# An encoder block on one Trainium2 core: the sums that seven-product pairs share move from SBUF into PSUM banks, and the step lists are rewritten around them

## The chip, the core and the metric

The kernel runs on one core of a Trainium2 chip. Five engines with queues of their own take part: TensorE (PE in the profile; PEld are its weight loads) multiplies out of SBUF into the eight banks of PSUM, VectorE (DVE) and ScalarE (ACT) do the elementwise work, GpSimd (POOL) here only issues DMAs that add to what lies in SBUF, and SyncE (SP) issues all other DMAs. Each engine goes through its instructions strictly in the order in which the program lists them; an instruction that waits holds up all behind it. The metric is the device time in microseconds, median of several runs.

## What is computed

One layer of a transformer-like encoder, on 256 tokens of width 2048, all in float32:

```
h     = rms_norm(x);  q,k,v of three mixers and three gates = h @ w_in
a,b,c = dilated-window attention, grouped attention with rotary, cross-attention into 256 memory tokens
x     = x + (sum over i of sigmoid(gate_i) * (branch_i @ w_br_i)) @ w_o
x     = x + (silu(hf[:, :5632]) * hf[:, 5632:]) @ w_ffn_out,   hf = rms_norm(x) @ w_ffn_in
```

Nearly all of the work is products of a 256-row activation with weights that are read once from memory (295 MB in all). To keep float32's precision on TensorE, every operand is split into a high part (`whi`, `xh`) and the rest (`wlo`, `xl`), and every product of a 128x128 block of activations with a 128x512 block of weights is made of three matmuls: high by high, high by low, low by high.

## The kernel before

Weights arrive in blocks of two K-blocks by 512 columns (512 KB), over SP's queue, in eight places called `raw`. For each block ACT copies the high part (`whi`, line 397) and DVE subtracts it for the low part (`wlo`, line 407), 128x1024 elements each. `halves` takes the two from five buffers in turn, so the high part of a step cannot be made before TensorE has finished the step five before it.

The large products go two column blocks at a time, as a "pair" (`pair`, line 409): column blocks c=0 and c=1, two token blocks of 128, and eight or more pairs of K-blocks. Most pairs of K-blocks are done plainly, as "wholes": step `d` (for c=0) or `D` (for c=1) is one 512 KB block, 12 matmuls. The others are done as "sevens": a 2x2x2 block product by seven block multiplications in place of eight, with sums of activations (`forms`, made once for each activation and kept) and sums of weight blocks. Each pair has four result chains that grow in PSUM (mmY, mmV, mmZ, mmQ) and two shared chains: mmX, to which the products with three different sums are added one after the other, and mmW. After each of three phases mmX is copied by ACT into SBUF (tiles SA and SB, line 448); the shared sums are made there by DVE (lines 552, 555), and at the end of a pair DVE adds them to the four chains (`sums`, line 456), before the gate's sigmoid, the silu or the residual addition reads them. Sums of weights are made 512 wide by DVE (lines 506, 507, 513, 529) into tiles t2 and t3; the addition of the first two blocks is a DMA that POOL issues and that accumulates 256 KB into a loaded block (line 485).

The stages in order of time: memory keys and values (0 to 51 us), the projection to queries, keys and values with attention beside it (to 286), the first gate products (to 314), `merging` (to 580; pairs of gates, each followed by the branch products that they multiply), `projecting` (to 670; w_o in two pairs), `feeding` (to 1364; eleven pairs for the FFN's input in three groups of 4, 4 and 3, and after each group two pairs for its output). In a pair of `feeding`, `hidden` takes silu of one column block, multiplies it with the other, and transposes the product on TensorE (tiles `tp`) for the output pairs.

What sets the order: a list of steps for each kind of pair, such as `STEPS_FFN`, is a string of step names. `run` walks through it: it emits the high part's copy of a step four steps ahead of its products, the low part one step behind the high part, and after each step `tick` lets side jobs (evacuations, transposes, activation sums) emit a piece. `nc.follow` keeps ACT's and DVE's weight work in that order. PSUM's eight banks are two tags of four in one pool.

## Time and profile before

| | |
|---|---|
| runs (3) | 1368.52, 1368.80, 1369.07 us; median 1368.8 |
| the profiled execution's span | 1368.0 us |
| PE busy | 1358.7 us (99%), 6195 instructions |
| DVE busy | 1190.5 us (87%), 1652 instructions |
| ACT busy | 865.4 us (63%) |
| DMA | 298.86 MB, mean 218 GB/s |
| granted TensorE clock | full in each of 40 slices |

The profiled execution is as long as the runs within 0.1%. Matmuls are pipelined: a record lasts 0.39 us while the next begins 0.23 us later, so "busy" says only that TensorE never stood still for long; how fast it goes is read from the spacing of the starts.

### The profile page before, as it was taken

To read this page: it belongs to the slowest core of one execution; us is meant where nothing else is said; L and a number is where in the kernel's file an instruction comes from. 1 tells how busy PE (TensorE), PEld (TensorE's weight loads), DVE (VectorE), ACT (ScalarE), POOL (GpSimd) and SP (SyncE) were. 2 spreads that over 40 slices of the span, in tenths; PEclk is the share of its full clock that TensorE was granted. 3 is DMA by queue.
4 is the path that set the end of the run, shared out by engine and by line. 5 is a ranking of instruction groups with operands and counts; after the bars stand their busy time and mean duration, and the time that the engine had idled before them with its cause. 6 is when DMAs were issued, how large, how long until landed. Compare 5 with 4: busy or idle time off the path is not lost.

```text
span 1368.0 us, 17866 instructions
## 1 busy us (share of the span) xinstructions
PE 1358.7 (99%) x6195; PEld 1125.7 (82%) x6195; DVE 1190.5 (87%) x1652; ACT 865.4 (63%) x1152; POOL 85.1 (6%) x97
## 2 busy tenths in 40 slices
PE   9999999999999999999999999999999999999998
PEld 7888888888888888887878888888888888888887
DVE  6868877759889888878999998989999989899998
ACT  7777665646665565656776666655666765566754
POOL 0010000000000100000000010000001000011000
PEclk9999999999999999999999999999999999999999
DMA  9976445557776775954777777777787767787673
GB/s 366 343 234 203 151 156 168 171 166 225 239 237 201 225 242 180 308 181 146 242 223 220 233 211 221 220 246 212 222 247 218 230 187 243 217 247 225 204 224 108
DMA packets 91674, 298.86 MB, mean 218 GB/s; under 512 B 10368, under 2 KB 12928, under 8 KB 91328
## 3 DMA queue, kind: packets, MB, share of 16 engines
q1 hardware_dynamic: 79488, 275.94, 60.2%
q0 software_dynamic: 11952, 21.76, 9.7%
q8 instruction: 48, 0.79, 0.2%
q14 instruction: 42, 0.34, 0.1%
q10 hardware_dynamic: 144, 0.02, 0.0%
HBM read 294.81 MB, written 2.88 MB: 218 GB/s over the span
## 4 chain that ended last, share of the span: by engine, by line
PE 86%; DVE 8%; issue 2%; DMA 2%; ACT 1%; SPq 0%; DVEq 0%; ACTq 0%
PE mm L77 16%; PE mmZ L77 14%; PE mmV L77 14%; PE mmY L77 14%; PE mmQ L77 11%; PE mmX L77 10%; DVE wlo L407 4%; PE mmW L77 3%; DMA raw<-in_w_ffn 2%; PE tp L77 1%; ACT whi L397 1%; PE sc L77 1%; PE o L77 1%; DVE t L506 1%; PE pT L77 1%
## 5 line engine op out<-in xcount | busy, mean ns | idle before, releaser
L397 ACT ACTIVATE whi<-raw 128x1024 fp32r<-128x1024 f32 (+1 forms) x460 | 479.4, 1051 | 350.6 <-PE mmV L77 109.6
L407 DVE TENSOR_TENSOR wlo<-raw,whi 128x1024 fp32r<-128x1024 f32 (+1 forms) x460 | 546.8, 1210 | 80.7 <-ACT whi L397 77.5
L77 PE MATMUL mm<-whi,xT 128*128 128x512 f32 x640 | 202.5, 393 | 0.0
L131 DVE TENSOR_TENSOR wlo<-raw,whi 128x1024 fp32r<-128x1024 f32 x82 | 102.1, 1248 | 43.6 <-ACT whi L130 42.9
L77 PEld LDWEIGHTS mm<-whi,xT 128*128 128x128 f32 x640 | 119.3, 188 | 23.5 <-issue 0.4
L130 ACT ACTIVATE whi<-raw 128x1024 fp32r<-128x1024 f32 x82 | 86.7, 1061 | 62.3 <-PE mm L77 45.4
L77 PE MATMUL mm<-wlo,xT 128*128 128x512 f32 x320 | 125.7, 393 | 0.0
L407 DVE TENSOR_TENSOR wlo<-t,whi 128x1024 fp32r<-128x1024 f32 x90 | 102.2, 1138 | 13.4 <-ACT whi L397 12.9
L397 ACT ACTIVATE whi<-t 128x1024 fp32r<-128x1024 f32 x90 | 89.0, 990 | 25.5 <-PE mmQ L77 11.4
L77 PE MATMUL mmX<-whi,forms 128*128 128x512 f32 x312 | 104.9, 389 | 0.0
L77 PE MATMUL mmY<-whi,x1T 128*128 128x512 f32 x266 | 96.7, 394 | 0.8 <-DVE x1T L134 0.8
L77 PE MATMUL mmV<-whi,x1T 128*128 128x512 f32 x266 | 91.3, 390 | 0.0
L77 PEld LDWEIGHTS mm<-wlo,xT 128*128 128x128 f32 x320 | 60.2, 188 | 12.3 <-issue 0.7
L77 PEld LDWEIGHTS mmX<-whi,forms 128*128 128x128 f32 x312 | 58.6, 188 | 12.3 <-ACT SB L448 0.2
L485 POOL DMA_DIRECT2D raw<-in_w_ffn x43 | 37.2, 865 | 441.0 <-DMA raw<-in_w_ffn 143.3
L77 PE MATMUL mmZ<-whi,x1T 128*128 128x512 f32 x180 | 63.0, 391 | 0.0
L77 PE MATMUL mmQ<-whi,x1T 128*128 128x512 f32 x180 | 62.8, 390 | 0.0
L77 PE MATMUL mmW<-whi,forms 128*128 128x512 f32 x156 | 61.6, 395 | 0.0
L77 PE MATMUL mmZ<-whi,forms 128*128 128x512 f32 x156 | 60.9, 390 | 0.0
L77 PE MATMUL mmX<-wlo,forms 128*128 128x512 f32 x156 | 60.8, 389 | 0.0
L77 PEld LDWEIGHTS mmY<-whi,x1T 128*128 128x128 f32 x266 | 50.0, 188 | 11.3 <-DVE x1T L134 1.2
L507 DVE TENSOR_TENSOR t<-t,raw 128x512 f32<-128x512 f32 x83 | 57.1, 688 | 1.6
(285 smaller groups left out, 2837.9 us busy)
## 6 DMA issues: line engine op xcount, KB each, us to landing
raw<-in_w_ffn SPq DMA_DIRECT2D x176, 512.0 KB, 4.7
raw<-in_w_gate SPq DMA_DIRECT2D x96, 512.0 KB, 4.4
raw<-in_w_ffn_out SPq DMA_DIRECT2D x88, 512.0 KB, 4.6
raw<-in_w_qkv SPq DMA_DIRECT2D x64, 512.0 KB, 4.3
raw<-in_w_o SPq DMA_DIRECT2D x32, 512.0 KB, 4.8
raw<-in_w_br SPq DMA_DIRECT2D x24, 512.0 KB, 4.2
raw<-in_w_ffn POOLq DMA_DIRECT2D x43, 256.0 KB, 5.5
raw<-in_w_mem SPq DMA_DIRECT2D x15, 512.0 KB, 8.3
```

The source lines that it names most:

```text
L77: ins = op(*args, **kw)
L130: nc.scalar.activation(hi, src, AF.Copy)
L131: nc.vector.tensor_sub(lo, src, hi.bitcast(F32))
L397: nc.follow(nc.scalar.activation(hi[:, o], v, AF.Copy))
L407: nc.follow(nc.vector.tensor_sub(*due.pop(0)))
L485: nc.gpsimd.dma_start(out=b2[:, 0], in_=src(u, 0)[:, :NC], accum_op=ALU.add)
L506: nc.follow(nc.vector.tensor_add(s2, b2[:, 0], b2[:, 1]))
L507: nc.follow(nc.vector.tensor_sub(s3, s2, b1[:, 0]))
```

## The change

Seven-product pairs get a new plan. Sevens now come in doubles (four sevens to a pair, two in the w_o pairs), and every step of a double handles the same phase of two sevens: step kinds X, W, P, Y, Q, Z, H, each one 128x1024 block of weights or of their sums and 6 matmuls; `l` and `r` start loads. The shared sums stay in PSUM. When the last X step is through, ACT copies mmX into the bank that becomes mmY (line 514); when the last W step is through, ACT copies mmW to SBUF (`m5`, line 517); when the last P step is through, DVE writes m5 minus mmX back into mmW (line 519); when the last Q step is through, DVE writes m5 minus mmX into a new bank mmQ (line 523). The four banks mmY, mmX, mmW, mmQ are then the results, the chains go on on top, and readers (sigmoid, silu, residual) read PSUM directly. Tiles SA and SB and their additions are gone. The sums of weights are 128x1024 wide on DVE (lines 537, 539, 541), and the accumulating DMA is 512 KB (line 495): 46 issues for 83.

Each pair has three lists: front, back, end. The column block c=1 (mmW, mmQ) is finished within the pair; the end list holds wholes of c=0 (mmY, mmX) that fill the places marked "." in the next pair's front. The number of sevens is larger than before: the program has 27 matmuls of 128x512 fewer for products, and 2 more that only mark the two copied banks in the first such pair. A new PSUM pool over the same eight banks is opened before that pair: four banks for c=0, two for c=1, two for transposes. There are eleven `raw` places instead of eight. The activations' sums are made for four K-blocks at a time, and those of the first activation earlier, beside the second gate product.

```diff
-STEPS_GATE = "d4 d0 D0 f1 g1 d5 D5 f2 d6 g2 D4 f3 h1 g3 p0 p2 D6 q0 h3 q2 d7 D7".split()
-STEPS_FFN = "d0 D0 d1 D1 f2 f3 d5 g2 D5 g3 h2 f4 d6 g4 p0 p2 h4 D6 q0 q2 d7 D7".split()
...
+STEPS_GATE = ("l0 l1 X0 . X1 . . r0 W0 r1 W1 P0 P1 . Y0 Y1 . Q0 Q1 .", "Z0 Z1 D4 H0 D5 H1 d4 D6 d5 D7 d6 d7", "")
...
+STEPS_FFN = ("l0 l1 X0 X1 . r0 W0 r1 W1 P0 P1 . Y0 Y1 . Q0 Q1 .", "Z0 Z1 D4 H0 D5 H1 D6 D7", "d4 d5 d6 d7")
+STEPS_LAST = ("l0 l1 X0 X1 . r0 W0 . r1 W1 . P0 P1 . Y0 Y1 Q0 Q1", "Z0 Z1 H0 H1 D4 D5", "d4 d5")
...
     def bank(name, tag="at"):
-        return psum.tile([P, NC], F32, name=name, tag=tag)
+        return psum[0].tile([P, NC], F32, name=name, tag=tag, bufs=2 if tag in ("c1", "tp") else 4)
...
-        def copy(to, b):
-            with tc.high_priority():
-                nc.scalar.activation(tl[to[0]][:, to[1]], ps[b], AF.Copy)
-
-        def sums(c):
-
-            if not seven or parts:
-                return [ps[b] for b in ("YV", "ZQ")[c]]
-            to = tl["AB"[c]]
-            for t in range(T):
-                nc.vector.tensor_add(to[:, t], ps[("YV", "ZQ")[c][t]], to[:, t])
-            return to
+        def ending():
+            for c, (a, b) in enumerate(("YX", "WQ")):
+                if left[a] == left[b] == 0 and c not in ended:
+                    ended.add(c)
+                    with tc.high_priority():
+                        done(c, [ps[a], ps[b]])
...
+        def begin(m):
+
+            j = doubles[m][0]
+            t1 = load((src(j, 1),), 0, PK)
+            raws[m] = {"b11": load((src(j, 0),), 0, PK), "t": t1}
+            nc.gpsimd.dma_start(out=t1.rearrange("p k n -> p (k n)"), in_=src(j, 0), accum_op=ALU.add)
...
+        def phase_end(kind, hi):
+            seen[kind] = seen.get(kind, 0) + 1
+            if seen[kind] < nd:
+                return
+            with tc.high_priority():
+                if kind == "X":
+                    new("Y")
+                    wake("Y", hi)
+                    nc.follow(nc.scalar.activation(ps["Y"], ps["X"], AF.Copy))
+                elif kind == "W":
+                    raws["m5"] = s4([P, NC], "m5")
+                    nc.follow(nc.scalar.activation(raws["m5"], ps["W"], AF.Copy))
+                elif kind == "P":
+                    nc.follow(nc.vector.tensor_sub(ps["W"], raws["m5"], ps["X"]))
+                elif kind == "Q":
+                    new("Q")
+                    wake("Q", hi)
+                    nc.follow(nc.vector.tensor_sub(ps["Q"], raws["m5"], ps["X"]))
+
+        def seventh(kind, m):
+            of = {"X": "b11", "W": "t", "Y": "b21", "P": "t", "Z": "b22", "Q": "b11", "H": "b21"}[kind]
+            bk = {"P": "X", "Q": "X", "H": "X", "Z": "W"}.get(kind, kind)
...
+                if kind == "P":
+                    nc.follow(nc.vector.tensor_add(raw, raw, r["b22"]))
+                elif kind == "Q":
+                    nc.follow(nc.vector.tensor_sub(raw, r["t"], raw))
+                elif kind == "H":
+                    nc.follow(nc.vector.tensor_add(raw, r["t"], raw))
+                hi, lo = halves(raw)
...
+            for front, back, end in pairs:
+                for s in front:
+                    if s is not None:
+                        yield s
+                    elif tail:
+                        yield tail.pop(0)
+                yield from tail
+                yield from back
+                tail = end
...
+    psum[0] = ctx.enter_context(tc.tile_pool(name="psum2", bufs=4, space=bass.MemoryType.PSUM))
...
-                    for t in range(T):
-                        nc.scalar.activation(r[:, t], r[:, t], AF.Sigmoid, scale=r_x[:, 0, t:t + 1])
+                    sg[c] = s4([P, T, NC], "sg")
+                    for t in range(T):
+                        nc.scalar.activation(sg[c][:, t], r[t], AF.Sigmoid, scale=r_x[:, 0, t:t + 1])
...
-                def hidden(c, v, av=halves_of, late=late if n == c1 - 1 - last else []):
-                    if c == 0:
-                        av.append(v)
+                def hidden(c, v, av=av, n=n - c0, hT=hT):
+                    if c == 1:
+                        av.append(s4([P, T, NC], "av"))
                         for t in range(T):
-                            nc.scalar.activation(v[:, t], v[:, t], AF.Silu, scale=r_f[:, 0, t:t + 1])
+                            nc.scalar.activation(av[0][:, t], v[t], AF.Silu, scale=r_f[:, 0, t:t + 1])
                         return
```

Three places of the program show how the instructions are ordered now. A number behind a name tells tiles of one name apart.

The first place is the border between the first and the second FFN input pair. On ACT before, the silu (line 916) reads SA in SBUF, which the shared sums have gone into; `scales` is the row scale of the FFN's norm:

```order
L397 ACTIVATE whi_6697<-raw_6695 128x1024
L448 ACTIVATE SA_6597<-mmX_6474 128x512
L397 ACTIVATE whi_6711<-raw4_6680 128x1024
L397 ACTIVATE whi_6733<-raw6_6731 128x1024
L916 ACT_TABLE_LOAD
L916 ACTIVATE SA_6597<-SA_6597,scales_111 128x512 x2
L397 ACTIVATE whi_6755<-raw2_6753 128x1024
L397 ACTIVATE whi_6775<-raw0_6678 128x1024
```

On ACT in the changed kernel the silu (line 924) reads mmW_6159 and mmQ_6318, the finished c=1 banks of the first pair, and stands behind the high part of step d7 (whi_6529):

```order
L413 ACTIVATE whi_6498<-raw2_6407 128x1024
L514 ACTIVATE mmY_6508<-mmX_6490 128x512
L413 ACTIVATE whi_6511<-raw5_6411 128x1024
L413 ACTIVATE whi_6529<-raw4_6527 128x1024
L924 ACT_TABLE_LOAD
L924 ACTIVATE av_6480<-mmW_6159,scales_111 128x512
L924 ACTIVATE av_6480<-mmQ_6318,scales_111 128x512
L413 ACTIVATE whi_6540<-raw1_6462 128x1024
```

DVE writes `scales` right behind the low part of that same step d7, where P's weight sums and low parts stand ahead of it:

```order
L537 TENSOR_TENSOR raw5_6411<-raw5_6411,both_3325 128x1024
L423 TENSOR_TENSOR wlo_6499<-raw2_6407,whi_6498 128x1024
L145 SCALAR_TENSOR_TENSOR rs_t_6370<-rs_y_6366 128x2
L423 TENSOR_TENSOR wlo_6512<-raw5_6411,whi_6511 128x1024
L146 TENSOR_TENSOR rs_t_6370<-rs_t_6370,rs_v_6354 128x2
L147 SCALAR_TENSOR_TENSOR rs_y_6371<-rs_t_6370,rs_y_6366 128x2
L423 TENSOR_TENSOR wlo_6530<-raw4_6527,whi_6529 128x1024
L156 COPY scales_111<-rs_y_6371 128x2
L157 TENSOR_TENSOR scales_111<-rs_y_6371 128x2
L423 TENSOR_TENSOR wlo_6541<-raw1_6462,whi_6540 128x1024
```

What moved: the reader of `scales` now holds a PSUM bank. TensorE's step W0 of the second pair (mmW_6533) begins in the bank of mmW_6159, so it stands behind that silu, and it comes before step d7 on TensorE.

The second place is the front of the first gate pair of `merging`, on DVE. Before, a stretch of it reads (t2 and t3 are sums of weights, forms and fraw sums of activations):

```order
L407 TENSOR_TENSOR wlo_3465<-raw5_3339,whi_3464 128x1024
L797 TENSOR_TENSOR fraw_3427<-fraw_3427,ffull_3424 128x128
L407 TENSOR_TENSOR wlo_3484<-raw_3481,whi_3483 128x1024
L529 TENSOR_TENSOR raw1_3319<-t2_3315,raw1_3319 128x512
L407 TENSOR_TENSOR wlo_3500<-raw4_3435,whi_3499 128x1024
L506 TENSOR_TENSOR t2_3315<-raw3_3433 128x512
L131 TENSOR_TENSOR forms_3305<-fraw_3398,forms_3305 128x512
L798 TENSOR_TENSOR fraw_3427<-fraw_3427,ffull_3424 128x128
L507 TENSOR_TENSOR t3_3316<-t2_3315,raw4_3435 128x512
L407 TENSOR_TENSOR wlo_3511<-raw1_3319,whi_3510 128x1024
L407 TENSOR_TENSOR wlo_3529<-raw3_3433,whi_3528 128x1024
L407 TENSOR_TENSOR wlo_3539<-t2_3315,whi_3538 128x1024
```

In the changed kernel the front holds these rows (mg1 is the first branch's product with its gate; raw rows are sums of weights for the steps P and Q):

```order
L806 TENSOR_TENSOR mg1_2849<-mm_3289,sg_3285 128x512
L537 TENSOR_TENSOR raw0_3327<-raw0_3327,raw4_3344 128x1024
L423 TENSOR_TENSOR wlo_3357<-raw2_3332,whi_3356 128x1024
L537 TENSOR_TENSOR raw2_3332<-raw2_3332,raw6_3352 128x1024
L423 TENSOR_TENSOR wlo_3362<-raw0_3327,whi_3361 128x1024
L423 TENSOR_TENSOR wlo_3374<-raw2_3332,whi_3373 128x1024
L423 TENSOR_TENSOR wlo_3387<-raw5_3346,whi_3386 128x1024
L539 TENSOR_TENSOR raw1_3329<-raw0_3327,raw1_3329 128x1024
L423 TENSOR_TENSOR wlo_3398<-more0_3354,whi_3397 128x1024
L539 TENSOR_TENSOR raw3_3334<-raw2_3332,raw3_3334 128x1024
L423 TENSOR_TENSOR wlo_3411<-raw1_3329,whi_3410 128x1024
L519 TENSOR_TENSOR mmW_3390<-m5_3407,mmX_3365 128x512
```

What moved: all activation sums have gone from here, and between the products of the first gates and the turning point of the shared chain (mmW_3390 from m5 and mmX_3365, which step Q0 waits for) stand seven low parts, four 1024-wide sums and that subtraction. This pair has no wholes of an earlier pair to fill its front.

The third place is a later gate pair, on DVE, where the branch products before it are multiplied with their gates and added up (sg, mg). Before, three low parts stand between the last addition to SB and the products with the gates:

```order
L456 TENSOR_TENSOR SB_3942<-mmQ_3791,SB_3942 128x512
L407 TENSOR_TENSOR wlo_4098<-raw5_4095,whi_4097 128x1024
L407 TENSOR_TENSOR wlo_4118<-raw1_4115,whi_4117 128x1024
L407 TENSOR_TENSOR wlo_4141<-raw4_4092,whi_4140 128x1024
L837 TENSOR_TENSOR SA_3941<-mmY_4101,SA_3941 128x512
L837 TENSOR_TENSOR SA_3941<-mmV_4108,SA_3941 128x512
L843 TENSOR_TENSOR mg0_2848<-mg0_2848,SA_3941 128x512
L843 TENSOR_TENSOR mg1_2849<-mg1_2849,SA_3941 128x512
L407 TENSOR_TENSOR wlo_4163<-raw0_4160,whi_4162 128x1024
L506 TENSOR_TENSOR t2_4088<-raw_4090 128x512
L837 TENSOR_TENSOR SB_3942<-mmZ_4121,SB_3942 128x512
L837 TENSOR_TENSOR SB_3942<-mmQ_4128,SB_3942 128x512
```

In the changed kernel these rows lie around the turning point, which reads m5_4155:

```order
L423 TENSOR_TENSOR wlo_4115<-more0_3964,whi_4114 128x1024
L849 TENSOR_TENSOR mg1_2849<-mg1_2849,sg_4002 128x512
L423 TENSOR_TENSOR wlo_4135<-raw6_4132,whi_4134 128x1024
L423 TENSOR_TENSOR wlo_4146<-raw1_4056,whi_4145 128x1024
L539 TENSOR_TENSOR raw3_3961<-raw0_3959,raw3_3961 128x1024
L423 TENSOR_TENSOR wlo_4158<-more1_4078,whi_4157 128x1024
L519 TENSOR_TENSOR mmW_4138<-m5_4155,mmX_4047 128x512
L539 TENSOR_TENSOR both_3325<-more0_3964,both_3325 128x1024
L843 TENSOR_TENSOR sg_4038<-mmY_4118,sg_4038 128x512
L423 TENSOR_TENSOR wlo_4169<-raw3_3961,whi_4168 128x1024
L843 TENSOR_TENSOR sg_4038<-mmX_4125,sg_4038 128x512
L849 TENSOR_TENSOR mg0_2848<-mg0_2848,sg_4038 128x512
```

What moved: the products with the gates (lines 843, 849) now fall between the sums and low parts of steps P, Y and Q, where before they fell between the wholes and the first sevens of the next pair.

More of the change, by code (lines that the diff above doesn't have):

```diff
@@ L285, in transposed @@
                 yield lag
-            tp = bank("tp", "mm" if h and nc.on else "at")
+            tp = bank("tp", "tp")
             for k in range(2):
@@ L562, in pair @@
-        kinds = {"d": lambda u: whole(u, 0), "D": lambda u: whole(u, 1), "f": first, "g": second, "h": third,
-                 "p": lambda v: rest("p", v), "q": lambda v: rest("q", v)}
-        steps = [kinds[o[0]](int(o[1:])) for o in order]
-        for i, ready in enumerate(steps):
-            for o in order[i:i + AHEAD + 1]:
-                if o[0] == "f" and int(o[1:]) not in begun and (o is order[i] or len(free) > 4):
-                    begun.add(int(o[1:]))
-                    fetch_both(int(o[1:]))
-            products = ready()
-            if i + 2 < len(steps):
-                yield products
-                continue
-            def ending(products=products, c=i + 2 - len(steps)):
-                products()
-                with tc.high_priority():
-                    done(c, sums(c))
-            yield ending
+                            mul(("YX", "WQ")[c][t], at(2 * u + k, t), hi[:, k], lo[:, k])
@@ L581, in run, with step, steps @@
+        def step(o):
+            if o == ".":
+                return None
+            kind, n = o[0], int(o[1:])
+            if kind in "dD":
+                return whole(n, "dD".index(kind))
+            if kind in "lr":
+                return lambda: (begin if kind == "l" else begin2)(n)
+            return seventh(kind, n)
+        return [[step(o) for o in l] for l in lists]
     def run(pairs, ahead):
         nc.on = True
-        waiting = []
-        for p in pairs:
-            for products in p:
-                low(1)
-                waiting.append(products)
-                if len(waiting) > ahead:
-                    waiting.pop(0)()
-                    tick()
+        def steps():
+            tail = []
+            for front, back, end in pairs:
[7 more added lines that the diff above has]
+                tail = end
+            yield from tail
@@ L593, in run @@
+        waiting = []
+        for ready in steps():
+            products = ready()
+            if products is None:
+                continue
+            low(1)
+            waiting.append(products)
+            if len(waiting) > ahead:
+                waiting.pop(0)()
+                tick()
         low(0)
@@ L773, in encoder_block, with gate_forms @@
     mg = [s8([P, D], f"mg{t}", F32) for t in range(T)]
+    form_room = lambda n: [s8([P, 2, 2, 4, P], "forms") for _ in range(n)]
+    gforms = []
+    def gate_forms():
+        yield 4
+        gforms.extend(form_room(2))
+        for g in range(2):
+            full = s4([P, 2, 4, P], "ffull")
+            hi, lo = (xT.tiles[g][:, :, i].rearrange("p (h i) s -> p h i s", i=2).bitcast(F32) for i in range(2))
+            nc.vector.tensor_add(full.rearrange("p i (h t) s -> p h i (t s)", t=T), hi, lo)
+            yield 2
+            token_sums(full, gforms[g])
+            yield 4
     for j in range(2):
+        if j:
+            start(gate_forms())
         n0 = j * NC
@@ L871, in add @@
                 for t in range(T):
[L872 removed]
+                    nc.vector.tensor_add(xc[t], r[t], xc[t])
+                ended.append(n + c)
+                last = len(ended) == 4
                 def later():
@@ L940, in feeding @@
+            pairs = (STEPS_LAST, STEPS_LAST2) if last else (STEPS_OUT, STEPS_OUT2)
             for n in (0, 2):
                 def output(c, r, n=n, last=last):
+                    final = last and n == 2 and c == 0
+                    w = NC // 2 if final else NC
                     for t in range(T):
-                        rt = r[t] if last else r[:, t]
-                        for h in range(2 if last and n + c == 3 else 1):
-                            w = NC if not (last and n + c == 3) else NC // 2
+                        for h in range(NC // w):
```

288 lines of the change are left out of this document (116 added, 172 removed).

## The prediction

> **What bounds the kernel now.** I read the page's engine rows and slices first, then the waits of TensorE, then its spacing.
>
> ```profile
> PE 1358.7 (99%) x6195; PEld 1125.7 (82%) x6195; DVE 1190.5 (87%) x1652; ACT 865.4 (63%) x1152; POOL 85.1 (6%) x97
> PE   9999999999999999999999999999999999999998
> DVE  6868877759889888878999998989999989899998
> PE 86%; DVE 8%; issue 2%; DMA 2%; ACT 1%; SPq 0%; DVEq 0%; ACTq 0%
> ```
>
> TensorE is busy in every slice and carries 86% of the chain that ended last. DVE has the second place: nine tenths in much of the second half.
>
> ```profile
> PE idle L77 <- POOL ident masks.py:199: 1.4, 1, 1.4
> PE mmY L77 <- DVE wlo L407: 1.3, 2, 1.0
> PE mmZ L77 <- DVE wlo L407: 1.0, 3, 0.4
> PE mmY L77 <- DVE x1T L134: 0.8, 1, 0.8
> PE tp L77 <- DVE SA L924: 0.6, 1, 0.6
> ...
> 7.74 0.51 PE L77 MATMUL mmY<-wlo,memT 128*128 128x512 f32 x1 [0.23 <-DVE wlo L407]
> 10.36 0.50 PE L77 MATMUL mmZ<-wlo,memT 128*128 128x512 f32 x1 [0.25 <-DVE wlo L407]
> ```
>
> These are all of TensorE's waits (total, times, longest): after the first matmul 3.7 us, in seven pauses, all on DVE. So two things can move the time: the number of matmuls, and pauses that the new order brings or takes away.
>
> ```profile
> 499.63 0.39 PE L77 MATMUL mmY<-whi,xT 128*128 128x512 f32 x1
> 499.86 0.39 PE L77 MATMUL mmY<-wlo,xT 128*128 128x512 f32 x1
> ...
> 502.35 0.39 PE L77 MATMUL mmZ<-whi,xT 128*128 128x512 f32 x1
> ```
>
> From 499.63 to 502.35 twelve matmuls start: 0.2267 us each. A step of a seven (6 matmuls) takes 1.36 us, a whole (12) 2.72. A record outlasts the next start by 0.39 - 0.23 = 0.16 us: after a pause that is lost too.
>
> **DVE's pace.** The new order stands or falls with it.
>
> ```profile
> 445.65 3.50 DVE L407 TENSOR_TENSOR wlo<-raw,whi 128x1024 fp32r<-128x1024 f32 x3
> 449.06 0.69 DVE L555 TENSOR_TENSOR SB<-SB,SA 128x512 f32<-128x512 f32 x1
> 449.66 0.68 DVE L456 TENSOR_TENSOR SA<-mmY,SA 128x512 f32<-128x512 f32 x1
> 450.26 1.22 DVE L407 TENSOR_TENSOR wlo<-raw,whi 128x1024 fp32r<-128x1024 f32 x1
> ...
> L924 DVE TENSOR_TENSOR SA<-SA,SB 128x1024 f32<-128x1024 f32 x11 | 13.4, 1218 | 0.0
> L507 DVE TENSOR_TENSOR t<-t,raw 128x512 f32<-128x512 f32 x83 | 57.1, 688 | 1.6
> ```
>
> Back to back, a low part takes (449.06 - 445.65) / 3 = 1.14 us, a 512-wide operation 0.60, from PSUM or not. The 1024-wide sum of line 924 has a record of 1.22 us like a low part's, so I give the new sums 1.14. A step of a seven with a sum thus costs DVE 2.28 us against TensorE's 1.36; a whole costs it 1.14 against 2.72. Over a pair that evens out, and DVE's whole load falls (138 sums of 1.14 us for 249 of 0.60 is about even; the 104 operations on SA and SB go). But a high part can be made only when the step five before it is through, so a front of sevens without wholes between runs at DVE's pace once that lead is eaten.
>
> **What is removed.** 25 matmuls fewer in all: 5.7 us. Of the pauses the two at the start stay (0.23 and 0.25). The other five sit at places whose order is gone: 3.2 us idle and five times 0.16, 4.0 us. If the two longest came back, 2.2 of it would.
>
> **The silu that now holds a bank.** The first place shown of the order: W0 of the second FFN pair needs the bank that silu reads; silu needs `scales`; that waits on DVE behind the low part of d7, and ACT has d7's high part ahead too. By the rule of five, d7's high part needs the end of d6, and d6 is the step just before W0. From W0's due time:
>
> ```profile
> 712.07 1.07 ACT L397 ACTIVATE whi<-raw 128x1024 fp32r<-128x1024 f32 x1 [0.90 <-PE mmV L77]
> 713.15 1.28 ACT L916 ACT_TABLE_LOAD   x1
> 714.45 1.34 ACT L916 ACTIVATE SA<-SA,scales 128x512 f32<-128x512 f32 x2
> ...
> 696.10 0.16 DVE L156 COPY scales<-rs_y 128x2 f32<-128x2 f32 x1
> ```
>
> 0.16 for the last matmul, 1.07 high part, 1.22 low part, 0.16 copy, 0.72 for one silu (1.34 for two that overlap), about 0.1 for the hand-overs: **3.4 us**. The table load (1.28) lies beside low part and copy. Bounds: 3.1 if the low part's overlap helps, 4.6 if the load comes after the copy. Behind silu on ACT stand the high parts from Y0 on, due 8 us later.
>
> [...]
>
> **The gate pairs' fronts.** These are the only fronts with both few wholes and DVE work of their own.
>
> First gate pair (second place shown). No wholes fill its front. Before the low part of W0, ACT has the two sigmoids of the gate product, which end one 12-matmul branch step before this pair: 2.72 - 0.3 - 1.34 - 1.07 leaves W0's low part to start about 0.2 us before X0 is due. From there DVE has, until the subtraction that Q0 waits for, seven low parts (8.0), four sums (4.6), two gate products (1.2) and itself (0.7): 14.5, so it ends at 14.3. TensorE is due at Q0 after eight steps and a marking matmul, 11.1. With 0.4 us that I find lost to ACT's order (the copy to mmY ahead of Y0's high part), 3.6 us, of which about 2.3 come at once, as X0's new bank waits for mg1. Bounds: 1.0 (0.16, mg1's 0.69, hand-over) to 4.5 (if the sigmoids end 1 us later).
>
> Second gate pair: two wholes. The sigmoids of the pair before wait for its last whole: 0.2 + 1.34, then W0's high part: DVE starts at 2.5. Seven low parts, four sums, four gate products (2.4) and the subtraction: 15.7, ends at 18.2. Q0 is due after eight steps and two wholes, 16.3: 1.9 us (0 to 2.6).
>
> Third and fourth: four wholes, but DVE's gate products are eight (4.8). From 2.6, thirteen low parts (14.8), five sums (5.7), those eight and the subtraction (0.6) end at 28.6 with the low part of D4, which is due after twelve steps and four wholes, at 27.4: 1.2 us each (0 to 1.7). The fifth has six wholes and comes out ahead. Together **7.9 us**.
>
> **Banks and the last pair.** With two banks for c=1, W0 after three wholes in a row waits for DVE's first gate product. In the fifth gate pair it starts at 10.6 behind five low parts and ends at 11.2, W0 is due at 10.9; in the first w_o pair 9.95 against 9.5. With the last matmul's overhang **0.8 us** (0 to 1.5). The first output pair of the last group has Y0 to H1 without a whole: DVE's subtraction for mmQ stands behind H0's low part and two sums and ends 9.5 after the last whole, H0 is due at 8.7: **0.9 us** (0 to 2).
>
> **Costed at nothing.** The pairs of `feeding`: after the last whole of c=1, silu ends 1.6 us later and W0 is due at 5.4; the subtraction before Q0 ends about 7 us ahead, as three wholes stand in the front; the closest is the product that the transposes read, 0.9 ahead. The copies at the turning points:
>
> ```profile
> L448 ACT ACTIVATE SA<-mmX 128x512 f32<-128x512 f32 x48 | 28.2, 587 | 7.5 <-PE mmX L77 7.5
> raw<-in_w_ffn SPq DMA_DIRECT2D x176, 512.0 KB, 4.7
> raw<-in_w_ffn POOLq DMA_DIRECT2D x43, 256.0 KB, 5.5
> ```
>
> 0.59 us behind at most one high part (1.07), covered by W0 and W1 (2.72); without that cover 0.8 us in each of 24 pairs. A 512 KB accumulation takes between 5.5 us and twice that, with the load before it 10 to 16; eleven steps or more, over 15 us, stand between. The plain loads have seven steps in `feeding` where they had three, which is why the pauses on late loads go.
>
> **The sum.** 1368.0 - 5.7 - 4.0 + 3.4 + 7.9 + 0.8 + 0.9 = 1371.3 for the profiled execution. The median of the runs lies 0.8 above its span: **1372.1 us**, 0.24% slower. With the pauses at their lower bounds (4.1) 1363.2, at their upper (18.0) 1377.1.
>
> **Rivals.**
>
> *Faster: DVE keeps ahead in the gate pairs.*
>
> ```profile
> 350.00:400.00 50.00, 50.00 (x222) 41.42 (x221) 46.37 (x52) 33.00 (x37) 3.42 (x4) 1.00 0.77 237
> 400.00:450.00 50.00, 50.00 (x223) 41.41 (x222) 44.61 (x51) 30.45 (x33) 3.44 (x4) 1.00 0.71 210
> ```
>
> For it: before, in `merging`, DVE (46.37 and 44.61 us of 50; the columns are the length, then PE, PEld, DVE, ACT and POOL busy) works 89 to 93% of the time without one pause of TensorE. It needs the sigmoids or high parts ahead of the fronts to end 2 us earlier than I read. Then silu's 3.4 and mg1's 1.0 are left: 1368.0 - 9.7 + 4.4 + 0.8 = 1363.5. Against it: the low parts were spread over wholes there.
>
> *Slower by much: every pair waits for its banks at W0.* c=1 has two banks for what it had four for, and W0 of each pair begins in the one whose reader is ACT. If silu or sigmoid came 4.2 us later than I read (so that the 3.8 us between 1.6 and 5.4 are gone), say behind four high parts that wait for loads, it would cost 0.4 us in each of the 22 other pairs: 1381. For it: ACT waited up to 5.9 us for loads before; against: those had three steps.
>
> ```profile
> ACT whi L397 <- DMA raw<-in_w_ffn: 28.2, 10, 5.9
> ```
>
> [...]
>
> *No change:* the pauses in the gate pairs at half of what I read: 1368.1.
>
> **Chances.** The forecast 0.55 (own range 1369 to 1377), the faster rival 0.30, much slower 0.08, no change 0.07. A measurement of this kernel tells about 0.2% (2.7 us) from nothing: faster is below 1366.1, slower above 1371.5. Of the forecast I put 0.34 above that line and 0.21 below; of the faster rival 0.25 clears it. Faster 0.25, same 0.33, slower 0.42. The range of 8 in 10 is 1363 to 1377, the bounds of the pauses; it reaches to the faster rival and leaves out the much slower one.
>
> **What would show it.** In the waits of TensorE: about 3 us on a bank whose releaser is silu, at the second FFN pair, and not in the others; a mmX of the first gate pair waiting for mg on DVE, then mmX waits on the subtraction of line 519 in the first two gate pairs; low parts late by 1 us in the third and fourth; nothing of the kind in the 19 later pairs. DVE's busy time some 60 us lower. It is wrong if `merging` shows no pause above 0.5 us (then the faster rival), or if waits recur in `feeding`.

## The result

| | before | changed |
|---|---|---|
| runs beside each other (4 and 4), median | 1368.66 us | 1375.03 us |
| lowest to highest | 1368.37 to 1369.07 | 1373.56 to 1375.88 |
| span of the profiled execution | 1368.0 us | 1371.8 us |

The ratio is 1.0044, with a 95% interval of 1.003 to 1.0058: the change makes the kernel slower by 0.44%. The forecast was 1372.1 us, slower, range 1363 to 1377.

From the profile page of the changed kernel its engine rows and the shares of the chain that ended last, then its waits of TensorE (total, times, longest):

```profile
PE 1355.9 (99%) x6170; PEld 1121.2 (82%) x6170; DVE 1154.8 (84%) x1411; ACT 852.1 (62%) x1101; POOL 53.2 (4%) x60
...
PE 93%; DVE 5%; issue 1%; ACT 1%; POOL 0%; DVEq 0%; ACTq 0%; POOLq 0%
```

```profile
PE mmW L77 <- ACT av L924: 3.3, 1, 3.3
PE mmX L77 <- DVE mmW L519: 2.3, 2, 1.2
PE mmX L77 <- DVE mg L806: 1.6, 1, 1.6
PE idle L77 <- POOL ident masks.py:199: 1.4, 1, 1.4
PE mmW L77 <- DVE wlo L423: 1.2, 2, 0.6
PE mmW L77 <- DVE sg L843: 0.9, 2, 0.4
PE tp L77 <- DVE mg L849: 0.6, 1, 0.6
PE mmX L77 <- DVE mmQ L523: 0.5, 1, 0.5
```

There are 25 matmuls fewer and 241 operations on DVE fewer, and of the pauses of before only those at the start are left. In their place stand those that this list names, and they are longer: the silu that holds a bank (3.3), the first two gate pairs (1.6 and 2.3), the low part of D4 in the third and fourth (1.2), the two bank hand-overs (sg, 0.9), H0 of the last group (0.5). Of this list only the transposes of the merged rows (tp, 0.6) were not forecast.

The largest one, in the timeline around the second FFN pair, on ACT, DVE and TensorE:

```profile
714.83 1.06 ACT L413 ACTIVATE whi<-raw 128x1024 fp32r<-128x1024 f32 x1 [0.71 <-PE mmX L77]
715.91 1.28 ACT L924 ACT_TABLE_LOAD   x1
717.26 0.69 ACT L924 ACTIVATE av<-mmW,scales 128x512 f32<-128x512 f32 x1
...
715.92 1.23 DVE L423 TENSOR_TENSOR wlo<-raw,whi 128x1024 fp32r<-128x1024 f32 x1 [0.28 <-ACT whi L413]
717.07 0.16 DVE L156 COPY scales<-rs_y 128x2 f32<-128x2 f32 x1
...
714.36 0.39 PE L77 MATMUL mmX<-whi,x1T 128*128 128x512 f32 x1
718.00 0.80 PE L77 MATMUL mmW<-whi,forms 128*128 128x512 f32 x1 [3.25 <-ACT av L924]
718.60 0.63 PE L77 MATMUL mmW<-wlo,forms 128*128 128x512 f32 x1
719.02 1.05 PE L77 MATMUL mmW<-whi,forms 128*128 128x512 f32 x2
719.88 0.63 PE L77 MATMUL mmW<-wlo,forms 128*128 128x512 f32 x1
...
721.03 0.40 PE L77 MATMUL mmW<-wlo,forms 128*128 128x512 f32 x1
```

Link by link as it was worked out: the high part of d7, its low part, the copy of `scales`, and silu 0.07 us after the table load. From 714.36 to 718.00 are 3.64 us where 0.227 were due: 3.4 lost. But behind the pause something new shows: the matmuls from 718.60 on start 0.42 to 0.43 us apart, and only from 721.03 every 0.227 again. The windows of that stretch (length, busy time of PE, PEld, DVE, ACT and POOL, then the granted clock) say why:

```profile
713.00:718.00 5.00, 1.75 (x8) 1.13 (x6) 3.98 (x8) 4.14 (x5) 0.00 (x0) 0.95 0.02 7
718.00:721.00 3.00, 3.00 (x7) 2.42 (x8) 0.00 (x0) 0.53 (x1) 0.00 (x0) 0.52 0.49 175
721.00:724.00 3.00, 3.00 (x14) 2.44 (x13) 1.26 (x2) 2.67 (x4) 0.00 (x0) 1.00 0.00 0
```

For three microseconds TensorE had half its clock (0.52 in the window): 1.4 us more. The four runs of the changed kernel had spans of 1371.8, 1372.6, 1374.1 and 1373.9 at mean clocks of 0.999, 0.999, 0.997 and 0.997. The two longer ones fit two such stretches in place of one, an estimate from these means: 0.003 of 1374 us make 7 to 10 us at half clock, 0.001 make 1 to 4, rounding taken in. By it most of the spread of 2.3 us goes with the clock too.

### The profile page after: what moved, and what is told of

Read it like the earlier page. It is cut to its first block, busy times and chain, and to the rows that moved or that the text cites. A ratio compares the mean times of both kernels' runs of the same rounds, so it can differ in the third digit from the quotient of the medians.

```text
span 1371.8 us, 17290 instructions
## 1 busy us (share of the span) xinstructions
PE 1355.9 (99%) x6170; PEld 1121.2 (82%) x6170; DVE 1154.8 (84%) x1411; ACT 852.1 (62%) x1101; POOL 53.2 (4%) x60
## 4 chain that ended last, share of the span: by engine, by line
PE 93%; DVE 5%; issue 1%; ACT 1%; POOL 0%; DVEq 0%; ACTq 0%; POOLq 0%
PE mmX L77 28%; PE mmW L77 19%; PE mm L77 16%; PE mmY L77 14%; PE mmQ L77 11%; DVE wlo L423 3%; PE tp L77 1%; PE sc L77 1%; PE o L77 1%; PE pT L77 1%; DVE raw L539 1%; PE hT L77 0%; DVE sg L843 0%; ACT whi L413 0%; PE idle L77 0%
## 5 line engine op out<-in xcount | busy, mean ns | idle before, releaser
L413 ACT ACTIVATE whi<-raw 128x1024 fp32r<-128x1024 f32 (+1 forms) x359 | 372.2, 1054 | 227.8 <-PE mmQ L77 49.4
L423 DVE TENSOR_TENSOR wlo<-raw,whi 128x1024 fp32r<-128x1024 f32 (+1 forms) x359 | 432.4, 1217 | 94.5 <-ACT whi L413 91.4
L413 ACT ACTIVATE whi<-more 128x1024 fp32r<-128x1024 f32 x102 | 107.7, 1056 | 68.1 <-DVE more L539 17.5
L423 DVE TENSOR_TENSOR wlo<-more,whi 128x1024 fp32r<-128x1024 f32 x102 | 124.2, 1220 | 18.8 <-ACT whi L413 17.8
L413 ACT ACTIVATE whi<-both 128x1024 fp32r<-128x1024 f32 x92 | 97.2, 1057 | 66.0 <-issue 12.1
L423 DVE TENSOR_TENSOR wlo<-both,whi 128x1024 fp32r<-128x1024 f32 x92 | 112.0, 1221 | 19.3 <-ACT whi L413 18.5
L77 PE MATMUL mmX<-whi,x1T 128*128 128x512 f32 x352 | 120.9, 389 | 0.0
L77 PEld LDWEIGHTS mmW<-whi,forms 128*128 128x128 f32 x368 | 69.7, 190 | 19.8 <-ACT av L924 3.7
L77 PE MATMUL mmW<-wlo,forms 128*128 128x512 f32 x184 | 72.3, 393 | 0.0
L77 PE MATMUL mmX<-wlo,x1T 128*128 128x512 f32 x176 | 68.5, 389 | 0.0
```

Of the source, the lines that this page charges most:

```text
L77: ins = op(*args, **kw)
L413: nc.follow(nc.scalar.activation(hi[:, o], v, AF.Copy))
L423: nc.follow(nc.vector.tensor_sub(*due.pop(0)))
```

## The experiments

The first four ran together, beside the kernel before (21 runs, median 1368.78 us).

**The silu copied out of its banks.** In the first FFN pair only, ACT copies the two finished banks into `av` as soon as they are done, and silu follows in SBUF when `scales` is there.

```diff
-                            nc.scalar.activation(av[0][:, t], v[t], AF.Silu, scale=r_f[:, 0, t:t + 1])
+                            if first:
+                                nc.scalar.activation(av[0][:, t], v[t], AF.Copy)
...
+                        if first:
+                            nc.scalar.activation(av[0][:, t], av[0][:, t], AF.Silu, scale=r_f[:, 0, t:t + 1])
```

> At the end of the first FFN input pair ACT only copies the two finished c=1 banks to SBUF; their silu follows in SBUF once the row scale is there (two more ACT operations). The reader of the banks no longer waits for the row scale. Theory: the 3.4 us pause at the second FFN pair and the stretch of half-rate clock behind it (six spacings of 0.43 us, 1.4 us lost in the profiled execution) are one thing, the second caused by the first. Then both go: span about 1371.8 - 3.4 - 1.4 = 1367.0, no spacing of 0.43 us after the start-up, clock 1.000 in every run, and the runs lie within 1 us of each other where those of the changed kernel spread over 2.3. Rival: the clock dips for another reason at that time; then the dip and the spread stay and the span is about 1368.4.

Measured: 1368.86 us (11 runs, 1368.42 to 1369.38), ratio to before 1.0001 (0.9992 to 1.001), span 1367.6, granted clock 1.00 in the profile (0.999 in four of the eleven runs, as in some of the kernel before). The wait for av and the half-clock stretch are gone, a small new wait has come (0.3, a low part in the next steps):

```profile
PE mmY L77 <- DVE wlo L423: 0.3, 1, 0.3
```

6.2 us in the medians come from this one wait: 3.4 of the pause; the rest, 2.8, I put down to the clock behind it, an estimate (in the profile it was 1.4). The runs now lie 1.0 us apart in place of 2.3; that the clock alone made them differ is not shown, since the 21 runs of the kernel before, which has no such pause, lie 3.4 us apart.

**The sigmoids later.** The gate's sigmoids of column block c=0 come two steps later on ACT, behind the high part that they held up; by the prediction they are what lets DVE start late in the second to fourth gate pair.

```diff
+                    def sig():
+                        if c == 0:
+                            yield 2
...
+                            ins = nc.scalar.activation(sg[c][:, t], r[t], AF.Sigmoid, scale=r_x[:, 0, t:t + 1])
+                            if c == 0:
+                                nc.follow(ins)
```

> In the gate pairs the sigmoids of c=0 stand behind the high part of the step that comes five after the pair's last whole, instead of ahead of it; nothing else is moved. Theory: the pauses in the second, third and fourth gate pair come from the late start of DVE's work in the front, which those two sigmoids (1.34 us) set. Then the wait for the subtraction at the second gate pair (1.27 us from start to start) and the two waits for low parts at the third and fourth (0.78 each, about 1.0 with small ones beside) go, the one at the first gate pair (1.35) stays, and the span falls by about 3, to 1368.7. Rival: DVE has simply too much work between X0 and Q0; an earlier start is lost in its queue, and the pauses stay at 0.8 or more each.

Measured: 1373.36 us (5 runs), ratio 1.0032 (1.002 to 1.0045), span 1371.6. A miss. The pause of the second gate pair fell from 1.27 to 0.82 us and the hand-over in the fifth (0.59) went, but the pauses of the third and fourth stayed at 0.78, and silu's grew to 4.0 since TensorE came to it earlier. So the sigmoids do not set these places. DVE's timeline in the third pair of the changed kernel shows what does: from the second P sum at 413.44 to the low part of D4 at 433.00 it has 22 operations and not one pause. The operation just ahead has waited 0.38 us for the end of the branch products (first row), so an earlier sigmoid or low part does not let DVE begin this stretch sooner.

```profile
412.83 0.69 DVE L843 TENSOR_TENSOR sg<-mmW,sg 128x512 f32<-128x512 f32 x1 [0.38 <-PE mmW L77]
413.44 1.22 DVE L537 TENSOR_TENSOR more<-more,raw 128x1024 f32<-128x1024 f32 x1
...
423.19 0.69 DVE L519 TENSOR_TENSOR mmW<-m,mmX 128x512 f32<-128x512 f32 x1
...
433.00 1.21 DVE L423 TENSOR_TENSOR wlo<-both,whi 128x1024 fp32r<-128x1024 f32 x1
```

**A turning point without cover: X beside P.** In the 14 pairs with the usual list the second X step stands right before P0, so ACT's copy of mmX to mmY has nothing to hide behind.

```diff
-STEPS_FFN = ("l0 l1 X0 X1 . r0 W0 r1 W1 P0 P1 . Y0 Y1 . Q0 Q1 .", ...
+STEPS_FFN = ("l0 l1 X0 . r0 W0 r1 W1 X1 P0 P1 . Y0 Y1 . Q0 Q1 .", ...
```

> In the list of the FFN pairs after the first and of the first eight columns' output pairs (14 pairs), the second X step stands right before P0 instead of three steps ahead; W0 and W1 come one step earlier. So the copy of mmX to mmY has no cover. Theory: the distance hides a copy of 0.59 us, the overhang of 0.16 and at most a high part of 1.06 ahead of it on ACT: each of the 14 pairs then pauses at P0 by 0.9 to 1.9 us, waiting for ACT's mmY; span 1384 to 1399. Rival: the copy is hidden anyhow, because ACT is idle there and P0's own low part is later than the copy: no change, within 2 us of 1371.8.

Measured: 1393.28 us (2 runs), ratio 1.0178 (1.016 to 1.0197), span 1392.8: within the expected range, 21.0 us more than the changed kernel or 1.5 us a pair.

```profile
PE mmX L77 <- ACT mmY L514: 13.4, 14, 2.3
PE mmW L77 <- ACT av L924: 4.8, 1, 4.8
```

The wait is there in each of the 14 pairs, 0.96 us idle each; with the overhang of 0.16 that is 15.7 of the 21.0 us. Silu's pause is 1.5 longer, and a second half-clock stretch came behind the longest of the new waits (2.3 us; granted clock 0.59 from 769 to 773).

**All the late places moved.** Both edits above; W0 one whole later in the fifth gate pair and the first w_o pair; D4 and D5 ahead of H0 and H1 in the last group's first output pair; the transposes of the merged rows one step later.

```diff
-STEPS_O = ("l0 X0 . . r0 . W0 . P0 . Y0 . Q0", ...
+STEPS_O = ("l0 X0 . . r0 . . W0 . P0 . Y0 Q0", ...
-... "Z0 Z1 H0 H1 D4 D5", "d4 d5")
+... "Z0 Z1 D4 H0 D5 H1", "d4 d5")
```

> Both edits together (silu from a copy; late sigmoids), and four list edits: W0 of the last gate pair and of the first w_o pair behind one whole more, D4 and D5 before H0 and H1 in the first output pair of the last group, the transposes of the merged rows one step later. Theory: each pause is set by its own place, so they add up: 1371.8 - 4.8 (silu and clock) - 3.0 (gate pairs) - 1.2 (two bank waits) - 0.7 (transpose) - 0.7 (last group) = 1361.4; the pauses of the first gate pair (3.1) stay. That is about 0.4% faster than the kernel before. Rival: DVE is behind by a fixed amount, and what is taken away at one place comes back at the next: 1366 or more.

Measured: 1368.31 us (11 runs), ratio 0.9994 (0.9985 to 1.0003), span 1366.5. Of the 10.4 us hoped for, 5.3 came, nearly all of it silu's 3.4 and 1.4: the gate pairs keep 1.72 + 1.34, 0.82, 0.79 and 0.76, and three edits only moved a pause (a new wait for mmQ of 0.57 in the w_o pair, a low part of 0.69 in the last pair, the transposes 0.86 in place of 0.63). This is the rival's outcome (1366 or more).

**DVE's work taken out of the gate pairs.** The theory that was left: in these fronts it is the sum of DVE's work that counts. The sums for the Q steps, b12 + b22, are made by an accumulating DMA in the five gate pairs, on a second load of b12.

```diff
+            if qsum:
+                raws[m]["q"] = q = load((src(doubles[m][0], 1),), 0, PK)
+                nc.gpsimd.dma_start(out=q..., in_=src(j, 1), accum_op=ALU.add)
...
-                elif kind == "Q":
+                elif kind == "Q" and not qsum:
```

> In the five gate pairs the weight sums of the Q steps (two per pair, 1.14 us each on DVE) are no longer made by DVE: block b12 is loaded a second time and b22 is accumulated on it by a DMA that POOL issues, as the first sum of each double already is. Ten DVE sums go, ten loads and ten accumulations of 512 KB come. Theory after the run with the late sigmoids: in these fronts DVE works back to back from the first P sum to the low part of D4, so it is its sum of work that makes the pauses. Then 2.28 us less work stands ahead of each of these places: the wait for mg1 in the first gate pair stays (1.72 us), the pauses before Q0 in the first and second gate pair (1.35 and 1.27) go, and so do those at D4's low part in the third and fourth (0.78 each): 4.2 us in all, span 1371.8 - 4.2 = 1367.6. Rival A, the high parts (held back by the rule of five) or the end of the branch product set these places: the pauses in the third and fourth pair stay as they are, at most 2.6 us go. Rival B, the accumulations come too late behind the extra loads: new waits for DMA in the gate pairs, span above 1372.

Measured: 1369.01 us (8 runs), ratio to before 1.0006 (0.9994 to 1.0018), span 1366.6. All four pauses are gone, also those at D4; mg1's stays, and no wait for a DMA came, though the stage's DMA share rose from 0.68 to 0.83.

```profile
PE mmW L77 <- ACT av L928: 3.3, 1, 3.3
PE mmX L77 <- DVE mg L810: 1.6, 1, 1.6
...
PE mmW L77 <- DVE sg L847: 0.9, 2, 0.4
PE tp L77 <- DVE mg L853: 0.6, 1, 0.6
PE mmX L77 <- DVE mmQ L526: 0.5, 1, 0.5
```

**The additions into mg later.** Of the same theory, without taking work away: the additions of line 849 in the third and fourth gate pair come eight steps later.

```diff
-                        yield 1
+                        yield 9 if b == 1 else 1
...
+                            ins = nc.vector.tensor_add(m, m, sg[c][:, t])
+                            if b == 1:
+                                nc.follow(ins)
```

> In the third and fourth gate pair the four additions of the gated branch products into mg (line 849, 0.60 us each in SBUF) are put behind their due place: eight steps later, in DVE's order behind the low part of D4. DVE's total stays the same. Theory that DVE's back-to-back work between the first P sum and D4's low part makes the pauses there: three to four additions (1.8 to 2.4 us) leave the stretch, so both pauses of 0.78 us go and nothing else changes: span 1371.8 - 1.6 = 1370.2, give or take the stretch at half clock. If the high parts or the branch product's end set the place, both pauses stay at 0.78 and the span at 1371.8.

Measured: one run, 1374.67 us, span 1372.9. Both pauses are still there, at 0.65. By DVE's timeline only two of the four additions had come behind the low part of D4 (the first two still stand at 428.92, ahead of it), and of the 1.2 us so freed DVE lost 0.5 at once to a high part:

```profile
417.81 2.59 DVE L423 TENSOR_TENSOR wlo<-raw,whi 128x1024 fp32r<-128x1024 f32 x2 [0.53 <-ACT whi L413]
...
428.92 1.29 DVE L849 TENSOR_TENSOR mg<-mg,sg 128x512 f32<-128x512 f32 x2
```

So this run does not decide between the theories by itself. It shows that a high part stands close behind DVE's work as the next limit: here the shift within the front was worth 0.13 us a pair, while the work taken out of it removed the whole pause.

**Pauses made on purpose.** What slows the clock? POOL multiplies a small piece of the FFN product several times in a chain, and one more transpose, whose result the real ones overwrite, waits for it.

```diff
+                            nc.gpsimd.tensor_mul(scr, scr if i else av[0][:, 1, :P], row)
...
+                nc.tensor.transpose(tp[:, :P], first[:, :P], ident)
```

> Nothing of the computation changes; in seven FFN input pairs of feeding (second, third, fifth, sixth, seventh, ninth, tenth) TensorE is made to wait: POOL multiplies a 128x128 piece of the product by a row several times in a chain, into a tile of its own, and one more transpose reads it ahead of the real ones. With 0.5 us for one multiplication (760 ns for 256 columns, 1298 for 512: about 0.22 + 0.0021 a column) and 0.9 us of lead, the pauses are about 2.1, 2.6, 3.6, 4.6, 3.1, 5.6 and 7.1 us (6, 7, 9, 11, 8, 13, 16 multiplications). The question is after which of them the matmuls start every 0.43 us in place of 0.227, and for how long. [...] Theory B, it is not the pause but what comes with it at the silu (the table load, the change of banks): none of these seven pauses slows the matmuls behind it. Span by A: 1371.8 + 28.7 for the pauses + about 1.5 to 3 for each slow stretch; the DMAs have time to run ahead meanwhile, so no other wait is expected.

Measured: one run, 1446.22 us, span 1444.5. The pauses came out 1.7 to 3.1 times as long as meant (6.5 to 11.8 us beyond the usual spacing), as the first multiplications of each chain took about 1.27 us, not 0.5. Each of the seven was followed by 4 to 9 spacings of about 0.43 us (granted clock 0.50 from 788 to 791 and from 838 to 842, behind two of them); the pause at silu, 3.64 us from start to start as before, this time by none.

**Shorter pauses.** The same with 1 to 4 multiplications, and the Q sums of the gate pairs by DMA.

> As the run with the long pauses, but with 1, 2, 3, 2, 3, 4 and 1 multiplications in the chain; the start of the chain then took 1.6 us beyond 0.98 for each further one, so pauses of about 1.6, 2.6, 3.5, 2.6, 3.5, 4.5 and 1.6 us. The Q sums of the gate pairs come by DMA here, as in the run that tested that; the silu's pause of 3.4 us is left in. [...] Rival: the clock falls after any pause of some 2 to 3 us or more: then the two of 3.5 and the one of 4.5 are followed by starts every 0.427 us for 1 to 3 us, those of 1.6 are not, and those of 2.6 tell where the bound lies.

Measured: one run, 1401.52 us, span 1399.7. From the last start before a pause to the first behind it, and then: 1.73, 3.15 and 3.27 us, full speed; 3.61, 4.41, 4.56 and 6.16 us, half speed for 3 to 4.5 us; silu's 3.64, half speed. One of these as a window, behind the pause of 3.61 (from 821.21):

```profile
826.00:829.00 3.00, 3.00 (x8) 2.33 (x8) 2.49 (x3) 2.12 (x3) 0.00 (x0) 0.51 1.05 276
```

The clock was at half (0.51) behind a pause without silu's table load or banks: the chain has neither. The rival does not hold as put: behind pauses of 3.15 and 3.27 us the matmuls ran at full speed, behind one of 3.61 they did not. What decides between these is not shown.

**All that worked.** Silu copied first, Q sums by DMA in the gate pairs, the first w_o pair and the last group's first output pair, the sigmoids later, W0 one whole later in the first w_o pair; and DVE's two products of the first gates (line 806; `first_gates` holds the second) ahead of the low part of W0:

```diff
+                if fresh and kind == "W" and m == 1:
+                    g = first_gates[0].ins
+                    nc.before[g.engine] = g.name
```

> The changed kernel with the edits that took a pause away so far, together: the silu of the first FFN pair copied out of its banks first; the sums of the Q steps by accumulating DMA in the five gate pairs, and now in the first w_o pair and the first output pair of the last group too; the sigmoids of the later column block two steps later; W0 of the first w_o pair one whole later; and, new, DVE's two products of the first gates (mg) ahead of the low part of W0 of the first gate pair in place of behind it. From the pauses of the changed kernel: silu 3.4 and the 1.4 at half clock behind it go, the gate pairs' 1.35, 1.27, 0.78 and 0.78, the hand-overs' 0.59 and 0.59, H0's 0.67; of mg1's 1.72 the 0.9 goes that the low part took (1.14, less what DVE waits for TensorE's end). That leaves about 0.8 there, 0.63 at the transposes of the merged rows, 0.24 in the projections: span 1371.8 - 11.6 = 1360, runs about 1361.5, against 1368.7 before: 0.5% faster. If what is left of the pauses is set by something the single runs did not show (the high parts, the extra DMAs), new waits of 0.5 to 1 us appear and the span stays above 1363.

Measured: 1362.26 us (5 runs, 1361.3 to 1362.58) against 1368.21 before (9 runs): ratio 0.9959 (0.9945 to 0.9973), span 1359.5. It is 0.41% faster than the kernel before. What TensorE still waits for:

```profile
PE idle L77 <- POOL ident masks.py:199: 1.4, 1, 1.4
PE mmX L77 <- DVE mg L814: 0.9, 1, 0.9
PE tp L77 <- DVE mg L866: 0.6, 1, 0.6
PE mmX L77 <- ACT mmY L518: 0.5, 1, 0.5
```

The last of these is new. In the first gate pair, with W0 and W1 between X1 and P0, ACT's copy of mmX starts at 320.19, behind a high part that has waited 1.33 us for a P sum of DVE, and P0 starts 0.65 us late.

**The other turning point without cover: P beside Q.** On that kernel, in the same 14 pairs.

```diff
-STEPS_FFN = ("l0 l1 X0 X1 . r0 W0 r1 W1 P0 P1 . Y0 Y1 . Q0 Q1 .", ...
+STEPS_FFN = ("l0 l1 X0 X1 . r0 W0 r1 W1 . Y0 Y1 . P0 P1 Q0 Q1 .", ...
```

> On the fastest kernel so far (span 1359.5): in the 14 pairs that use the usual list of feeding (ten FFN input pairs, four output pairs) the steps P0 and P1 stand right ahead of Q0 instead of the two Y steps and a whole between them, so DVE's subtraction that turns the shared chain into mmW has nothing to hide behind; nothing else changes. Theory: the distance is what hides it. Without it Q0 waits in each of the 14 pairs for the subtraction: at least its 0.69 us with the last matmul's overhang of 0.16 (0.85), more where DVE still has the low parts and sums of Q0 and Q1 ahead of it (those are 4.6 us of work against 2.7 of TensorE in P0 and P1, so up to 2). Span 1371 to 1388, waits of mmX for DVE mmW 14 times. Rival: the turning points would be hidden anyway, by the order of DVE's work or because DVE is ahead: fewer than 5 such waits, span below 1363.

Measured: 1381.73 us (2 runs), ratio to before 1.01 (1.0071 to 1.0129), span 1380.9, 21.4 us or 1.5 a pair more.

```profile
PE mmX L77 <- DVE mmW L523: 15.9, 14, 2.3
```

All 14 pairs wait, 1.14 us on average; the first waits longest (2.3 us), and a half-clock stretch follows it (granted clock 0.50 from 726.06 to 729.47). Together with X beside P: in these pairs the three or four steps between a turning point and its next use (whole, W0, W1; whole, Y0, Y1, whole) are what hides the sums in PSUM; without them each of the two places costs a pair some 1.5 us of span.

## Why the prediction was right, and where it was not

The sign, the median within about 0.2% and nearly every pause were as forecast. The step from the kernel before was not: 6.4 us between the medians where 3.3 were forecast, and some 3 us of it I put down to the clock, by the estimate above (the 6.2 us that the copied silu gave back, less its 3.4). Term by term, the losses measured as spacing of the starts beyond 0.227 us:

| term | forecast | measured |
|---|---|---|
| 25 matmuls fewer | -5.7 | -5.7 (by count) |
| pauses of before | -4.0 (five) | -4.2 (those and one of 0.3) |
| silu holds W0's bank | 3.4 | 3.4 |
| first gate pair | 3.6 | 1.72 + 1.35 = 3.1 |
| second, third, fourth gate pair | 1.9, 1.2, 1.2 | 1.3, 0.8, 0.8 |
| bank hand-overs | 0.8 | 1.2 |
| H0 of the last group | 0.9 | 0.7 |
| half clock behind silu | none | 1.4 |
| transposes of merged rows, projections | none | 0.6 + 0.2 |
| sum | +3.3 | +3.6 |

The profiled span grew by 3.8. So the sum came out right partly by luck, because two errors cancel: the gate pairs were 1.9 us too dear, and the clock and the transposes were missing. The upper bounds of the pauses add up to 18.6 us, not 18.0, so the range should have ended at 1377.7.

*The silu.* Right in size and in each link: silu starts 0.07 us after the load of 1.28, and the pause is 3.4. What failed is what I took to lie behind the pause: nothing. The half clock costs 1.4 us more in this profile (none in the run with the long pauses, where behind the same pause of 3.64 us no spacing was longer); silu copied first removed both.

*The gate pairs.* Right that DVE's back-to-back work sets Q0 and D4, and the run with the Q sums by DMA shows it. Two parts of the step were wrong. DVE's start was put on the sigmoids; moved away, they changed the third and fourth pair by nothing. So the faster rival's condition ("the sigmoids or high parts ahead of the fronts to end 2 us earlier") was no way to it for the sigmoids; taking 2.28 us of work out of the front was. Why each term was some 0.5 too dear, ACT's timeline shows in the third pair:

```profile
404.67 0.69 ACT L838 ACTIVATE sg<-mmY,scales 128x512 f32<-128x512 f32 x1 [0.30 <-PE mmY L77]
406.03 0.69 ACT L838 ACTIVATE sg<-mmX,scales 128x512 f32<-128x512 f32 x1 [0.67 <-PE mmX L77]
406.62 2.00 ACT L413 ACTIVATE whi<-raw 128x1024 fp32r<-128x1024 f32 x2
```

The sum put both sigmoids (1.34) behind the last whole, which ends where X0 starts, at 405.83. But the one that reads mmY runs while TensorE still does the second half of that whole, so only one stands behind it. DVE's work begins at 407.70, 1.9 us behind X0 and not 2.5 or 2.6, and in the second pair it is 1.9 too. From there the work was sized well (15.5 us for 15.7 in the second pair, 25.9 for 25.9 in the third with 0.5 of waiting between). In the first pair DVE's low part of W0 starts 0.85 us ahead of X0's due time, not 0.2 (and the differences given for it make 0.0).

*The bank hand-overs, H0.* Within 0.4 and 0.2 of the forecast. Its own terms for the hand-overs, 0.3 and 0.45 with twice the overhang of 0.16, make 1.1 and not 0.8, against 1.2 measured. The transposes that read mg 0.6 us too early were not looked at, though line 849 stood in the third place of the order.

*Costed at nothing.* Right, but for the silu and H0 above: no other pair of feeding waits at its turning points, at W0, or for a load. But "without that cover 0.8 us in each of 24 pairs" was too cheap: 1.1 us a pair with the overhang at the copy, 1.3 at the subtraction, and 1.5 a pair in span with what followed.

*The rivals.* Faster did not happen. Much slower (a bank wait at W0 in every pair) did not either: three W0 of 24 wait, those whose reader is late for a reason of its own. In the other pairs of feeding W0 starts 4.7 to 5.9 us after the end of the operation that reads its bank, so two banks for c=1 were enough.

*DVE.* Its busy time fell by 35.7 us, not by some 60. The sums of weights are even as worked out (170.7 us before, 168.4 now, grouped by line), and for the 136 operations on SA and SB (93 us) came 48 subtractions into PSUM (33 us): 88 fewer, not 104. Added up one by one, DVE's records fell by 58 us. But busy time counts overlapping records once, and the overlap fell by 22 us: the low parts alone take 668.7 us for 553 where they took 649.3 for 550, as more of them stand alone, and fewer share the 0.08 us by which a record of 1.22 outlasts the 1.14 to the next start. That is record time, not a slower DVE.

*From span to runs.* I put the runs 0.8 above the span. In every run of both kernels that has a span beside its time the difference is 1.7 to 1.8: the profiled execution of before, 1368.0, was about 1 us longer than its timed runs, and 1368.8 belonged to spans near 1367. That is 1.0 of the 2.9 us between 1372.1 and 1375.0; 0.5 is the span, 1371.8 for 1371.3, and 1.5 is the distance from the profiled run (1373.6) to the median, in which the runs at the lower clock count.

## What to carry to other kernels

In the 14 usual pairs keeping shared sums in PSUM cost nothing with three or four steps between the write of a bank and its next use, and about 1.5 us at each place without them. The steps are time for the engine that makes the sum, not a guarantee: where it had work waiting ahead of it, TensorE waited all the same (Q0 of the first two gate pairs; P0 of the first gate pair in the kernel with all that worked). What made this change slower was a reader of a bank (silu) that waited for a late row scale, and fronts in which DVE had more work per step than TensorE. Count an engine's back-to-back work from its last wait up to the place where its result is due, and if it is too long take work out (another engine, a DMA); shifting it within the front gained little here. And take a pause of TensorE of 2.7 us or more as possibly dearer than its length: here half clock followed six of nine between 2.66 and 3.64 us and all thirteen from 4.2 us on.

## What the runs showed of the hardware

Behind some pauses of TensorE its clock was at half: in the changed kernel the granted clock was 0.50 from 717.45 to 720.87, behind the silu's pause of 3.64 us, and matmuls started every 0.427 us in place of 0.227. In the twelve profiles of this case, the start left aside, no pause of up to 1.95 us from start to start was followed by slower matmuls. Of nine between 2.66 and 3.64 us six were: 2.66 with P beside Q, 2.70 with X beside P, 3.61 among the shorter pauses, and three of the four silu pauses of 3.64; the fourth, in the run with the long pauses, and two of the shorter pauses, 3.15 and 3.27, were not. Of thirteen from 4.2 us on all were: the seven long ones, three of the shorter ones (4.41, 4.56, 6.16), and silu's in the runs with the later sigmoids, with X beside P and with the later additions. In the run with the shorter pauses the matmuls were slow for 3 to 4.5 us each time.

So length alone does not part the pauses between 2.66 and 3.64 us. Two of them as windows, each with the one behind it, from the run with X beside P (pause of 2.70 us) and the run with shorter pauses (3.27 us), in the columns used above, then the DMAs' share and GB/s:

```profile
766.00:769.00 3.00, 0.91 (x5) 0.41 (x3) 2.91 (x4) 3.00 (x5) 0.00 (x0) 1.00 0.00 0
769.00:773.00 4.00, 3.78 (x10) 2.95 (x11) 2.16 (x2) 2.19 (x3) 0.00 (x0) 0.59 0.45 131
...
1039.00:1043.00 4.00, 1.12 (x9) 0.70 (x7) 3.14 (x3) 0.00 (x0) 3.25 (x3) 1.00 1.01 262
1043.00:1046.00 3.00, 3.00 (x16) 2.50 (x14) 1.86 (x3) 2.74 (x4) 0.00 (x0) 1.00 1.06 273
```

Behind the shorter of the two the granted clock was 0.59, behind the longer 1.00. What makes the difference is not shown.

A multiplication of the chains on POOL (128x128, into the chain's own tile) took from 0.40 to 1.27 us: the median was 0.40 for the 63 in the run with the long pauses and 1.26 for the 9 in the run with the shorter ones. Why some took three times as long is not shown.
